# Merge gates of chunks 3 and 4: seven half-size products for all tokens, in place of eight for half of them

## The chip, the cores and the metric

The kernel runs on one core of one Trainium2 chip. The metric is the device time of one execution in microseconds (us), as the median of several runs; lower is better. The engines go by the names that the profile gives them: PE (TensorE, the matmuls; PEld is its weight load), DVE (VectorE), ACT (ScalarE), POOL (GpSimd) and SP (SyncE, which issues most of the DMAs).

## The reference

The reference is one encoder block over 2048 tokens of 1024 channels. Two attention mixers (`ya` and `yb` below) are left as they are; the change lies in the merge gates:

```python
h = rms_norm(x, norm_gain[layer])
proj = h @ w_in[layer]
qa, ka, va, qb, kb, vb, ga, gb, mg = jnp.split(proj, split_idx, axis=-1)
...
br_a = ya @ w_branch_a[layer]
br_b = yb @ w_branch_b[layer]
gates = jax.nn.sigmoid(mg.reshape(bsz, S, N_BRANCHES, D) + b_merge[layer])
merged = gates[:, :, 0] * br_a + gates[:, :, 1] * br_b
x = x + merged @ w_out[layer]
```

`mg` has 2 x 1024 columns: for each of the 1024 output channels two gates, one for each branch. So the merge gates are a product of x (2048 x 1024) with weights of 1024 x 2048.

## The kernel before

**Numbers in two halves.** Values are held as pairs of fp16 numbers, hi and lo, and a product is three matmuls: hi x hi, hi x lo, lo x hi. x lies in SBUF as `XH` and `XL`, with 8 chunks of 128 input channels on the partitions and 2048 tokens in the columns. Each x is used transposed, so a matmul gives 128 output channels by 512 tokens, a quarter of the tokens.

**The stage.** The change lies in the stage of the merge gates, which follows the attention units. The 1024 output channels are 8 chunks `dc`. Five of them are made here, as n = 0 to 4 (chunk n is `DCS[n + 1]`); the other three are made at other places of the kernel. Both gates of a chunk use its raw weights `wraw`, 1024 inputs by 256 columns.

Before anything is multiplied, the weights of a chunk are prepared (`prep`, `w_load` to `w_lo`, lines 188 to 258): four DMAs load them into `wraw`, of which there is only one buffer; POOL multiplies by the norm's gain (L193, four instructions); ACT squares and sums (L235, four); PE adds up the squares over the partitions (L210, one product of 4 columns, which stands in PE's own queue); DVE makes a power of two of the sum, in six small instructions (L217 to L225); ACT makes the hi half (L252) and DVE the lo half (L258).

There are two ways of multiplying:

- `gate_pair(n, q)` makes both gates of a chunk for one quarter q of the tokens: 2 x 24 matmuls of 512 columns (8 input chunks by 3; L333). ACT takes the tanh (L1403), SP stores it into `mgd` in DRAM.
- `gate_group(n)` makes both gates for quarters 0 and 2 at once, by Strassen's scheme in Winograd's form. It sees x as 2 x 2 blocks (quarter 0 or 2, by input chunks 0 to 3 or 4 to 7) and the weights as 2 x 2 blocks (by gate). Eight products of half-size blocks become seven, of 12 matmuls each (L1516), with the sums S1 to S4 of x and T1, T2, T3, N4 of the weights as operands. What comes out of PSUM goes through ACT's copies (L1521), DVE's scaled additions (L1524), POOL's additions (L1527) and ACT's tanh (L1530).

**Sums of x** (`x_sums`, L1435) are made once for quarters 0 and 2: for each pair of channels (c, c + 4) 16 steps, which are four whole values hi + lo (DVE, L1441), four additions or subtractions (DVE, issued from L433), four hi halves (ACT, L1444) and four lo halves (DVE, L1448). They lie in the tiles `wt` (`xsum`, L1424), with the working values in a tile `Y`. **Sums of the weights** (`w_sums`, L1460) overwrite the raw weights: a DVE subtraction (L1483), ACT's hi half (L1484), DVE's lo half (L1480). The last lo half of a chunk is the last reader of `wraw`; only after it can the next chunk be loaded.

**The order of the work.** The order in which instructions are issued is written out by hand. `at(t, f)` puts a step on a heap with a due time t, `job` issues matmuls on a clock of PE (2.6 us for 12) and `until` issues every step whose time has come between them. So the tables `T_P` (start of preparation and of the weights' sums of each chunk), `T_S` (sums of x), `T_O` (blocks of W_out for the kernel's end: `b_load`, L1342, and `b_blocks`, L1352), `T_G`, `T_H`, `T_Y` (loads and splits of Y, the mixers' output, for the next stage) set where a step stands on its engine. At run time each engine takes its instructions in that order and waits where an operand or a buffer isn't ready. The due times don't hold anything back.

In the stage, before, pairs and groups follow in this order (n, q; a group with its number of products): pairs (0, 1) and (0, 3), two products of group 0, pairs (1, 1) and (1, 3), five of group 0, group 1, pairs (2, 1) and (2, 3), groups 2, 3 and 4, then pairs (3, 1), (3, 3), (4, 1), (4, 3). The next stage multiplies Y by the branch weights, with the first matmul `fps<-Y,wh` at L333.

Of the kernel before, what the change touches and what calls it, by code (L numbers as in the profile page):

```python
# [27 lines left out]
OP = mybir.AluOpType  # L28
# [72 lines left out]
T_Y = (2.0, 0.8, 1.6, 1.5, 4.0, 26.0, 0.5, 1.3, 2.1, 1.6, 2.0)  # L101
T_P = ((0, 0.0, 0.03), (1, 3.0, 50.0), (2, 56.0, 75.0), (3, 82.0, 102.0), (4, 108.5, 128.3))
T_O = ((0, 62.0, 84.0), (1, 136.4, 154.0), (2, 136.9, 164.6), (3, 183.9, 190.0))
T_G = (143.4, 174.8, 176.0, 177.4)
T_S = (2.0, 11.0, 0.85, 1.6, 0.75, 1.5, 0.9, 1.3, 0.8)
T_H = (157.4, 2.0, 0.02)
T_GATE = (0.1, 0.1, 0.9, 1.0, 1.0)
T_W = (0.3, 5.5, 1.1, 8.5, 0.9, 15.6, 16.1, 17.0, 0.9, 0.8)
T_B = (20.0, 6.5, 1.55, 0.8)
T_BR = (7.0, 0.95, 20.0, 9.0, 34.0)  # L110
# [13 lines left out]
def block_kernel(tc, x, w_units, w_gate, w_mrg, w_brn, w_out, w_bra, gain, qkg, sink, bias_a, bias_b, b_merge, out):  # L124
# [1150 lines left out]
    ygs, ypool = {}, [(fg, 6, "fg")]  # L1275

    def y_load(c, q):
        ygs[c, q] = ypool[0][0].tile([128, 512], F32, name=ypool[0][2], bufs=ypool[0][1])[:]
        nc.sync.dma_start(out=ygs[c, q], in_=ytd[c][:, 512 * q:512 * q + 512])

    def y_hi(c, q):
        A.activation(YS[q][0][:, c, :], ygs[c, q], AF.Copy, scale=ys[c][:])

    def y_lo(c, q):
        V.scalar_tensor_tensor(YS[q][1][:, c, :], ygs[c, q], ys[c][:], YS[q][0][:, c, :], OP.mult, OP.subtract)
        done.add(("y", c, q))
# [55 lines left out]
    def b_load(j):  # L1342
        if j < 3:
            rv = y0.tile([128, 4, 512], F32, name=f"Y0{1 - j % 2}")[:]
        else:
            rv = raw_tile()[:].rearrange("p a b -> p (a b)")[:, :2048].rearrange("p (a b) -> p a b", b=512)
        for i in range(2):
            for h in range(2):
                nc.sync.dma_start(out=rv[:, 2 * i + h, :], in_=w_out[h, :, 4 * i + j, :])
        bw["out", j] = rv  # L1350

    def b_blocks(t0, j):  # L1352

        b11, b12, b21, b22 = (bw["out", j][:, k, :] for k in range(4))
        sub = {0: (b11, b12, b11), 1: (b12, b22, b12), 3: (b22, b22, b11), 5: (b21, b21, b22)}
        for i, (b, v) in enumerate(((B11, b11), (B22, b22), (B21, b21), (T1, b11), (T3, b12), (T2, b22), (N4, b21))):
            hi, lo = split(wt[0][:, b, j, :], wt[1][:, b, j, :], v, so4)
            at(t0 + T_B[2] * i, hi)
            at(t0 + T_B[2] * i + T_B[3], lambda lo=lo, b=b: (lo(), done.add(("b", j, b))))
            if i in sub:  # L1360
                at(t0 + T_B[2] * i + T_B[3] + .05, lambda o=sub[i]: V.tensor_tensor(*o, OP.subtract))
# [29 lines left out]

    def gate_pair(n, q):
# [5 lines left out]
        for k in range(2):  # L1398
# [11 lines left out]
            at(e + T_GATE[4], store)  # L1410

# [12 lines left out]
    def xsum(i, c):  # L1424
        m = 4 * i + c
        return [wt[k][:, m % 7, 1 + m // 7, :] for k in range(2)]

    def xblock(b, c):
        if b in sidx:
            assert ("xs", sidx[b], c) in done  # L1430
            return xsum(sidx[b], c)
        o = 1024 if b == A22 else 0
        return [X[:, c + (0 if b == A11 else 4), o:o + 512] for X in (XH, XL)]

    def x_sums(t, c):  # L1435
# [4 lines left out]
        def whole(o, ch, tok):  # L1440
            V.tensor_tensor(o, XH[:, ch, tok:tok + 512], XL[:, ch, tok:tok + 512], OP.add)  # L1441

        def hi(v, i):
            A.activation(xsum(i, c)[0], v, AF.Copy, scale=0.25)  # L1444

        def lo(v, i):
            h, l = xsum(i, c)
            V.scalar_tensor_tensor(l, v, 0.25, h, OP.mult, OP.subtract)  # L1448
            done.add(("xs", i, c))
# [39 lines left out]
    def gate_group(n):  # L1489
# [21 lines left out]
        def products(ps, x, bl):  # L1511
            mm = []
            for ch in range(4):
                for k, w in ((0, 0), (1, 0), (0, 1)):
                    i = len(mm)
                    mm.append(lambda ch=ch, k=k, w=w, i=i: T.matmul(  # L1516
                        ps[:], lhsT=weight(bl, ch)[w], rhs=xblock(x, ch)[k], start=(i == 0), stop=(i == 11)))
            return mm
# [10 lines left out]
        def gate(o, v, k, q, late):  # L1529
            at(now[0] + late, lambda: A.activation(o, v, AF.Tanh, bias=bmh[:, 8 * k + dc:8 * k + dc + 1], scale=ims[n][:]))  # L1530
# [26 lines left out]
    for c in range(4):  # L1557
        at(t + T_S[0] + T_S[1] * c, x_sums, t + T_S[0] + T_S[1] * c, c)
# [12 lines left out]
    for c in range(4):  # L1571
        at(t + T_H[0] + T_H[1] * c, y_ahead, c)

# [4 lines left out]
    y_part(t + T_G[3], 0, 2, 0.9)  # L1578
    group0 = gate_group(0)
# [7 lines left out]
    until(clock[0] + T_GATE[4] + .1)  # L1587
# [266 lines left out]
```

## Time and profile before

| what | us |
|---|---|
| three runs | 1916.34, 1916.52, 1917.65 |
| median | 1916.52 |
| profiled execution | 1917.63 |
| its span | 1915.7 |
| PE busy in the span | 1903.7 |
| DVE busy | 1358.8 |
| ACT busy | 1119.7 |
| POOL busy | 842.9 |

The span is the part of the execution that the profile covers. Times in the trace are counted from its start. The stage of the change runs there from 1407.12 (first matmul of pair (0, 1)) to 1601.60 (first matmul of the next stage). Below, s is the time since 1407.12. A row of the order of time on an engine gives start, duration, engine, line, operation, output and inputs with their shapes, how many alike follow each other (x2), and in brackets an idle time before it with what ended it. DVE and ACT overlap instructions that follow each other, so a duration may be longer than the distance to the next start.

### The profile page before, as it was taken

What the parts mean: (1) busy time and instruction counts of PE and PEld (TensorE: products, weight loads), DVE (VectorE), ACT (ScalarE), POOL (GpSimd) and SP (SyncE); (2) the same over time, 40 slices, a digit from 0 to 9 for tenths busy, and PEclk for the clock granted to TensorE, in tenths of its full rate; (3) what the DMA queues carried; (4) which work ended last, traced back from release to release, by engine and by line L of the source; (5) the groups of instructions that cost most, each with busy time, mean ns of one, the idle gap of its engine ahead of it and who ended that gap; (6) DMA issues with size and microseconds to landing.
All of it is one profiled execution on the core that took longest, in us unless ns stands there. A gap on an engine that the chain in (4) does not pass through costs nothing.

```text
span 1915.7 us, 39344 instructions
## 1 busy us (share of the span) xinstructions
PE 1903.7 (99%) x13614; PEld 1195.4 (62%) x13614; DVE 1358.8 (71%) x3513; ACT 1119.7 (58%) x2496; POOL 842.9 (44%) x1848
## 2 busy tenths in 40 slices
PE   8999999999999999999999999999999999999999
PEld 7556666677766688566787667876544444444444
DVE  6668886887767777567776878868686667867312
ACT  7558766786666677566776766666544545323100
POOL 2433444344445655546565565655412211223543
PEclk9999999999999999999999999999999999999999
DMA  7559987797958696678877887767722346788763
GB/s 269 140 90 176 206 162 155 146 192 157 200 98 191 134 194 131 120 155 173 170 134 149 161 176 146 138 118 131 187 76 97 107 154 220 223 253 254 259 229 140
DMA packets 624584, 316.56 MB, mean 165 GB/s; under 512 B 492928, under 2 KB 562176, under 8 KB 623104
## 3 DMA queue, kind: packets, MB, share of 16 engines
q1 hardware_dynamic: 605952, 305.39, 69.2%
q10 hardware_dynamic: 18432, 8.66, 1.9%
q8 instruction: 106, 1.74, 0.4%
q14 instruction: 94, 0.77, 0.2%
HBM read 129.91 MB, written 65.27 MB: 102 GB/s over the span
## 4 chain that ended last, share of the span: by engine, by line
PE 89%; DVE 4%; POOL 2%; issue 2%; ACT 2%; DMA 2%; SPq 0%; DVEq 0%; POOLq 0%; ACTq 0%
PE pj L709 40%; PE pj L333 15%; PE fps L333 11%; PE fps L1721 6%; PE s L879 5%; PE pv L928 4%; PE fps L1516 3%; PE pj L1721 2%; PE pj L1516 1%; PE pj L609 1%; DVE qss L753 0%; DVE pr L894 0%; DMA xt<-in_x_dram 0%; DMA kq<-spl 0%; POOL rw L771 0%
## 5 line engine op out<-in xcount | busy, mean ns | idle before, releaser
L709 PE MATMUL pj<-wh,XL 128*128 128x384 f16 x1792 | 586.1, 327 | 0.0
L709 PE MATMUL pj<-wh,XH 128*128 128x384 f16 x1792 | 584.5, 326 | 1.6 <-DVE vt L741 1.6
L709 PE MATMUL pj<-wl,XH 128*128 128x384 f16 x1792 | 584.7, 326 | 0.0
L709 PEld LDWEIGHTS <-XH 128*128 128x128 f16 x3584 | 410.4, 116 | 152.2 <-issue 2.2
L894 DVE CUSTOM_DVE_ANT_0 pr<-s,b,ubuf 128x256 f32<-128x256 f32 (+3 forms) x512 | 219.1, 465 | 76.7 <-PE s L879 75.1
L709 PEld LDWEIGHTS <-XL 128*128 128x128 f16 x1792 | 207.7, 116 | 70.3 <-issue 1.2
L911 DVE SCALAR_TENSOR_TENSOR p<-pr,p 128x512 f16<-128x512 f32 (+2 forms) x256 | 190.5, 744 | 20.3 <-ACT p L907 20.3
L786 POOL COPY spl<-spl 128x256 f16<-128x256 f16 (+1 forms) x224 | 88.1, 423 | 183.1 <-DVE spl L781 181.6
L726 ACT ACTIVATE rw<-pj 128x256 f32<-128x256 f32 (+1 forms) x224 | 86.6, 386 | 138.8 <-PE pj L709 126.2
L907 ACT ACTIVATE p<-pr 128x512 f16<-128x512 f32 (+2 forms) x256 | 159.2, 622 | 6.2
L333 PEld LDWEIGHTS <-wh 128*128 128x128 f16 x960 | 93.7, 98 | 110.6
L879 PE MATMUL s<-kq 128*128 128x256 f16 (+3 forms) x1168 | 147.8, 254 | 0.0
L928 PEld LDWEIGHTS <-pt 128*128 128x128 f16 x3024 | 125.4, 97 | 35.4 <-DMA pt<-p 0.7
L286 POOL TENSOR_TENSOR rs_t<-rs_y 128x8 f32<-128x8 f32 (+1 forms) x112 | 41.1, 367 | 234.4 <-DVE rs_y L278 185.3
L771 POOL TENSOR_TENSOR rw<-rw,g 128x256 f32<-128x256 f32 (+1 forms) x112 | 90.9, 811 | 109.9 <-DVE rw L765 73.3
L193 POOL TENSOR_TENSOR wraw<-wraw,gn 128x768 f32<-128x768 f32 (+1 forms) x80 | 112.2, 1409 | 55.0 <-DMA wraw<-in_w_mrg_dram 43.2
L928 PE MATMUL pv<-vt,pt 128*128 128x65 f16 (+1 forms) x3024 | 132.7, 192 | 0.3 <-DMA pt<-p 0.3
L879 PEld LDWEIGHTS <-kq 128*128 128x128 f16 x1184 | 101.9, 98 | 41.5
L741 DVE SCALAR_TENSOR_TENSOR vt<-pj,vt 128x128 f16<-128x128 f32 (+1 forms) x224 | 62.1, 277 | 91.2 <-ACT vt L735 87.5
L765 DVE TENSOR_TENSOR rw<-rw,qr 128x512 f32<-128x512 f32 (+1 forms) x112 | 103.8, 927 | 31.8 <-POOL qr L295 31.1
L333 PE MATMUL pj<-XH,gh 128*128 128x512 f16 x320 | 121.3, 379 | 0.0
L333 PE MATMUL pj<-XH,gl 128*128 128x512 f16 x320 | 121.2, 379 | 0.0
(281 smaller groups left out, 3803.2 us busy)
## 6 DMA issues: line engine op xcount, KB each, us to landing
wraw<-in_w_units_dram SPq DMA_DIRECT2D x56, 384.0 KB, 4.7
mtd<-mm SPq DMA_DIRECT2D x56, 256.0 KB, 3.9
M<-mtd SPq DMA_DIRECT2D x8, 1792.0 KB, 9.8
mgd<-fg SPq DMA_DIRECT2D x39, 256.0 KB, 2.1
zd<-z ACTq DMA_DIRECT2D x128, 66.0 KB, 2.5
zz<-zd SPq DMA_DIRECT2D x64, 132.0 KB, 2.8
xt<-in_x_dram SPq DMA_DIRECT2D x16, 512.0 KB, 9.8
gtd<-yo SPq DMA_DIRECT2D x32, 256.0 KB, 3.2
```

The costliest lines, as they stand in the source:

```text
L193: G.tensor_tensor(v, v, gn[:, c0:c0 + 2].unsqueeze(2).to_broadcast([128, 2, n]), OP.mult)
L333: out.append(lambda w=w, xx=xx, ch=ch, i=i: T.matmul(ps[:], lhsT=w[:, ch, c0:c0 + 128], rhs=xx[:, ch, ts], start=(i == 0), stop=(i == n - 1)))
L709: out.append(lambda lhs=lhs, rhs=rhs, ch=ch, k=k: T.matmul(ps[:, :384], lhsT=lhs[:, ch, :], rhs=rhs[:, ch, :], start=(k == 0), stop=(k == ...
L765: V.tensor_tensor(q, q, self.rr[:, :n].unsqueeze(2).to_broadcast([128, n, HD]), OP.mult)
L771: G.tensor_tensor(k, k, GT[un.br][:].unsqueeze(1).unsqueeze(1).to_broadcast([128, 2, un.nk, HD]), OP.mult)
L786: G.tensor_copy(sp[:, i, nh:, :, :], sp[:, i, nq:nh, ::-1, :])
L879: T.matmul(self.sv[j][:, o:o + k1 - k0], lhsT=q[:, h, qo:qo + 128], rhs=kt[:, un.nq + kh + v * un.nk, k0:k1], start=(v == 0), stop=(v == 1))
L894: V.tensor_tensor_reduce(out=self.pv[:, j, self.p0:self.p0 + W], in0=self.sv[j], in1=un.bias[:, self.h0 + j, self.b0:self.b0 + W], scale=I ...
L907: A.activation(self.sp[:, :128 * n], self.pr, AF.Copy, scale=PSC)
L911: V.scalar_tensor_tensor(self.sp[:, 128 * n:], self.pr, PSC, self.sp[:, :128 * n], OP.mult, OP.subtract)
L928: T.matmul(self.po[:, j, :w], lhsT=p[:, n * j + s, :], rhs=un.v[key][:, vh, c0:c0 + w], start=(k == 0 and s == 0), stop=(k == 2 and s == n ...
L1721: mm.append(lambda ch=ch, k=k, w=w, i=i: T.matmul(ps[:, :cols.stop - cols.start], lhsT=m[:, a, ch, k, :], rhs=wt[w][:, b, ch, cols], start ...
```

## The change

Chunks 3 and 4 get a second group each, for quarters 1 and 3 (`p = 1`), and lose their pairs. So for these two chunks all tokens go by seven products. Counted as whole ones of 512 columns there are 24 matmuls fewer in the stage (900 before); 48 of the new groups' are halves of 256 columns, so the number of PE's instructions stays.

- `x_sums`, `xblock` and `xsum` take p. For p = 1 there are 16 more sums, at 16 new places m = 16 to 31. Only 21 places are in `wt`; m = 21 to 31 lie in columns of `XH` and `XL` whose x isn't read any more (`dead` counts the uses). For m = 25 to 28 such a place is two pieces of 256 columns, in two channels; `pieces` cuts every instruction on them in two.
- The places in `wt` are numbered by channel first (4c + i), no longer by sum first (4i + c).
- The working values of Y's quarter 0 (`y_load`) and of block 2 of W_out (`b_load`) also go to such columns, so that the instructions on them (L1339 and L1340, Y's hi and lo halves, now L1361 and L1362) come in halves.
- The order of pairs and groups is a table, `SEQ`; the tables of due times have new numbers.

Lines move: L193 to L196, L210 to L213, L235 to L238, L433 to L436, L1403 to L1437, L1441 to L1489, L1444 to L1496, L1448 to L1501, L1480 to L1533, L1483 to L1536, L1484 to L1537, L1516 to L1573, L1521 to L1579, L1524 to L1582, L1527 to L1585, L1530 to L1589.

```diff
-T_P = ((0, 0.0, 0.03), (1, 3.0, 50.0), (2, 56.0, 75.0), (3, 82.0, 102.0), (4, 108.5, 128.3))
+T_P = ((0, 0.01, 0.01), (1, 4.24, 49.92), (2, 52.84, 74.95), (3, 81.2, 102.03), (4, 107.96, 128.8))
...
+T_X = ((0.11, 13.73, 27.24, 34.11), (48.57, 50.03, 69.09, 119.78))
+SEQ = ((0, 1, 0), (0, 3, 0), (0, 0, 2), (1, 1, 0), (1, 3, 0), (0, 0, 5), (1, 0, 7), (2, 1, 0), (2, 3, 0), (2, 0, 7), (3, 0, 7), (4, 0, 7), (3, 2, 7), (4, 2, 7))
+GROUPS = sorted({(n, q // 2) for n, q, _ in SEQ if q % 2 == 0})
...
+    def pieces(*views):
+        if any(isinstance(v, list) for v in views):
+            return [[v[k] if isinstance(v, list) else v[:, 256 * k:256 * k + 256] for v in views] for k in range(2)]
+        return [views]
...
     def b_load(j):
-        if j < 3:
-            rv = y0.tile([128, 4, 512], F32, name=f"Y0{1 - j % 2}")[:]
+        if j == 2:
+            assert all(dead(0, b, c) for b in (A11, A12) for c in range(4))
+            rv = [x_place(4 + k, 0) for k in range(4)]
...
-    def xsum(i, c):
-        m = 4 * i + c
-        return [wt[k][:, m % 7, 1 + m // 7, :] for k in range(2)]
+    def dead(p, b, c):
+        return uses[p, b, c] == 3 * sum(g[1] == p for g in GROUPS)
+
+    def xsum(p, i, c):
+        m = 4 * c + i + 16 * p
+        if m < 21:
+            return [wt[k][:, m % 7, 1 + m // 7, :] for k in range(2)]
+        if m < 25:
+            return [X[:, m - 21, 1024:1536] for X in (XH, XL)]
+        if m < 29:
+            return [[X[:, 2 * (m - 25) + k, S:S + 256] for k in range(2)] for X in (XH, XL)]
+        return [X[:, m - 29, 1536:2048] for X in (XH, XL)]
...
-        o = 1024 if b == A22 else 0
+        o = 512 * p + (1024 if b == A22 else 0)
         return [X[:, c + (0 if b == A11 else 4), o:o + 512] for X in (XH, XL)]
...
     def gate(o, v, k, q, late):
+            q += p
...
-    for c in range(4):
-        at(t + T_S[0] + T_S[1] * c, x_sums, t + T_S[0] + T_S[1] * c, c)
+    for p in range(2):
+        for c in range(4):
+            b = t + T_X[p][c]
+            at(b, x_sums, b, p, c)
...
-    for n, q in ((0, 1), (0, 3), (group0, 2), (1, 1), (1, 3), (group0, 5), (gate_group(1), 7), (2, 1), (2, 3),
-                 (gate_group(2), 7), (gate_group(3), 7), (gate_group(4), 7), (3, 1), (3, 3), (4, 1), (4, 3)):
-        if isinstance(n, int):
+    for n, q, k in SEQ:
+        if q % 2:
             gate_pair(n, q)
-        else:
-            for _ in range(q):
-                next(n)
+            continue
+        g = groups.setdefault((n, q), gate_group(n, q // 2))
+        for _ in range(k):
+            next(g)
```

What the new numbers move is shown at three places. The first is DVE from the end of the first sums of x on, among the sums of the weights of chunk 1. `wraw` are raw weights, `wl` and `yq` hold lo halves of the weights' sums, `fg` is a gate, `fps` PSUM, `Y` the working values of the sums of x, `wt_21885` and `wt_21886` the two tiles of their hi and lo halves, `ubuf` a scale. Before:

```order
L1448 SCALAR_TENSOR_TENSOR wt_21886<-Y_22232,wt_21885 128x512 x2
L1467 TENSOR_SCALAR ubuf<-ubuf 128x1
L1483 TENSOR_TENSOR wraw<-wraw 128x4x128
L1480 SCALAR_TENSOR_TENSOR wl<-wraw,ubuf,wh 128x4x128
L1483 TENSOR_TENSOR wraw<-wraw 128x4x128
L1524 SCALAR_TENSOR_TENSOR fg<-fps,wt_21885 128x512
L1480 SCALAR_TENSOR_TENSOR wl<-wraw,ubuf,wh 128x4x128
L1483 TENSOR_TENSOR wraw<-wraw 128x4x128
L1480 SCALAR_TENSOR_TENSOR yq<-wraw,ubuf,yq 128x512
L1524 SCALAR_TENSOR_TENSOR fg<-fps,fg 128x512
L1483 TENSOR_TENSOR wraw<-wraw 128x4x128
L1480 SCALAR_TENSOR_TENSOR yq<-wraw,ubuf,yq 128x512
```

After, the end of the same sums of the weights:

```order
L1536 TENSOR_TENSOR wraw<-wraw 128x4x128
L436 TENSOR_TENSOR Y_22328<-Y_22328 128x512
L1489 TENSOR_TENSOR Y_22344<-XH,XL 128x512
L1533 SCALAR_TENSOR_TENSOR wl<-wraw,ubuf,wh 128x4x128
L1501 SCALAR_TENSOR_TENSOR wt_21886<-Y_22328,wt_21885 128x512
L1536 TENSOR_TENSOR wraw<-wraw 128x4x128
L436 TENSOR_TENSOR Y_22344<-Y_22344 128x512
L1582 SCALAR_TENSOR_TENSOR fg<-fps,fg 128x512
L1533 SCALAR_TENSOR_TENSOR yq<-wraw,ubuf,yq 128x512
L1501 SCALAR_TENSOR_TENSOR wt_21886<-Y_22344,wt_21885 128x512
L436 TENSOR_TENSOR Y_22328<-Y_22328 128x512
L1533 SCALAR_TENSOR_TENSOR yq<-wraw,ubuf,yq 128x512
```

The second half's sums of channels 0 and 1 (the rows with `Y` and `wt`, L436, L1489 and L1501) now stand between the sums of the weights, so that the last row, the last reader of `wraw`, has many more instructions ahead of it.

The second is ACT around the squares of chunk 2 (L235, now L238). Before:

```order
L1484 ACTIVATE yq<-wraw,ubuf 128x512 x2
L1530 ACTIVATE fg<-fg,bmh,ubuf 128x512
L1530 ACTIVATE wt_21885<-wt_21885,bmh,ubuf 128x2x256
L1530 ACTIVATE fg<-fg,bmh,ubuf 128x512
L1521 ACTIVATE fg<-fps 128x512
L235 ACTIVATE wl,wsq<-wraw 128x2x256 x2
L1530 ACTIVATE fg<-fg,bmh,ubuf 128x512
L235 ACTIVATE wl,wsq<-wraw 128x2x256 x2
```

After:

```order
L1496 ACTIVATE wt_21885<-Y_22328 128x512
L1589 ACTIVATE fg<-fg,bmh,ubuf 128x512
L1496 ACTIVATE XH<-Y_22344 128x512
L1589 ACTIVATE wt_21885<-wt_21885,bmh,ubuf 128x2x256
L1496 ACTIVATE wt_21885<-Y_22328 128x512
L1589 ACTIVATE fg<-fg,bmh,ubuf 128x512
L1496 ACTIVATE XH<-Y_22344 128x512
L238 ACTIVATE wl,wsq<-wraw 128x2x256 x3
L1579 ACTIVATE fg<-fps 128x512
L238 ACTIVATE wl,wsq<-wraw 128x2x256
```

The hi halves of the new sums (L1496) now stand ahead of the squares, and each of them needs a value of DVE's.

The third is PE at the norm product of chunk 2 (L210, now L213; `ones` is a matrix of ones, `wsq` the sums of squares). Before, in product S3 of group 1:

```order
L1516 LDWEIGHTS wh
L1516 MATMUL fps<-wt_21885,wh 128x512
L210 LDWEIGHTS ones
L210 MATMUL fps<-wsq,ones 128x4
L1516 LDWEIGHTS wh
L1516 MATMUL fps<-wt_21886,wh 128x512
```

After, in product S2 of group 1, with the weights' sum T2 in `yq`:

```order
L1573 LDWEIGHTS yq
L1573 MATMUL fps<-wt_21885,yq 128x512
L213 LDWEIGHTS ones
L213 MATMUL fps<-wsq,ones 128x4
L1573 LDWEIGHTS yq
L1573 MATMUL fps<-wt_21886,yq 128x512
```

The norm product stands 15 matmuls earlier in PE's queue: 316 matmuls of the stage are ahead of it, and 331 were before.

More of the change, by code (lines that the diff above doesn't have):

```diff
@@ L1390, in block_kernel @@
     ims = {}
+    plain = {1: 0, 3: 0}
     def gate_pair(n, q):
@@ L1410, in gate_pair @@
             at(e + T_GATE[4], store)
+        plain[q] += 1
     def prep(t, u):
@@ L1515, in products, with product @@
                     i = len(mm)
-                    mm.append(lambda ch=ch, k=k, w=w, i=i: T.matmul(
-                        ps[:], lhsT=weight(bl, ch)[w], rhs=xblock(x, ch)[k], start=(i == 0), stop=(i == 11)))
+                    def product(ch=ch, k=k, w=w, i=i):
+                        parts = pieces(ps[:], xblock(p, x, ch)[k])
+                        for o, v in parts:
+                            T.matmul(o, lhsT=weight(bl, ch)[w], rhs=v, start=(i == 0), stop=(i == 11 and v is parts[-1][1]))
+                    mm.append(product)
             return mm
```

94 lines of the change are left out of this document (61 added, 33 removed).

## The prediction

> **What bounds the kernel now.** I read the profile's page first, then the stretches by engine, then the order of time on each engine. On the page, the busy line and the chain that ended last say the same: TensorE (PE) works 99% of the span and carries 89% of the chain.
>
> ```profile
> PE 1903.7 (99%) x13614; PEld 1195.4 (62%) x13614; DVE 1358.8 (71%) x3513; ACT 1119.7 (58%) x2496; POOL 842.9 (44%) x1848
> ...
> PE 89%; DVE 4%; POOL 2%; issue 2%; ACT 2%; DMA 2%; SPq 0%; DVEq 0%; POOLq 0%; ACTq 0%
> ```
>
> So a matmul taken away is time taken away, as long as nothing makes PE wait. The stage of the change is read from two PE rows: its first matmul and the first matmul of the next stage.
>
> ```profile
> 1407.12 0.38 PE L333 MATMUL fps<-XH,wh 128*128 128x512 f16 x1
> ...
> 1601.60 0.59 PE L333 MATMUL fps<-Y,wh 128*128 128x512 f16 x2
> ```
>
> The stage lasts 194.5 us. Before, it holds 900 matmuls of 512 columns and four tiny ones, so one takes 0.216 us and PE stands still nowhere. I count time in it as s, microseconds after 1407.12. The stretches (PE, PEld, DVE, ACT, POOL busy) show how close VectorE (DVE) is behind:
>
> ```profile
> 1420.00:1450.00 30.00, 30.00 (x141) 13.53 (x139) 29.64 (x52) 18.20 (x33) 2.12 (x2) 1.00 0.14 54
> 1450.00:1480.00 30.00, 30.00 (x141) 13.62 (x140) 13.18 (x24) 11.98 (x23) 8.78 (x7) 1.00 0.36 123
> ```
>
> While the sums of x are made, DVE is full (29.64 of 30); right behind that it is at 13 of 30. The change puts the second half of the sums there.
>
> **What goes.** Chunks 3 and 4 lose 4 x 48 matmuls of the plain pairs and get 2 x 84 of the groups: 24 fewer, 24 x 0.216 = 5.2 us. Of the 168, 24 come as 48 halves of 256 columns, because four sums lie in two pieces. The end of the kernel has both widths:
>
> ```profile
> L1721 PE MATMUL fps<-wt,M 128*128 128x512 f16 x24 | 5.3, 379 | 0.0
> L1721 PE MATMUL fps<-wt,M 128*128 128x256 f16 x24 | 2.8, 272 | 0.0
> ```
>
> 48 halves cost 5.6 us at this rate against 5.3 for 24 whole ones: between 0 and 0.3, I take 0.1.
>
> **What comes on DVE.** 48 more whole instructions for the sums, four of them cut in two. 36 of them are planned ahead of s 88, in the way of the weights of chunks 2 and 3: the sums of channels 0 and 1 at s 49 to 63, those of channel 2 at s 69 to 82, mixed with the sums of the weights of chunks 1 and 2. DVE works in order, so its queue can be added up.
>
> ```profile
> 1409.28 1.28 DVE L1483 TENSOR_TENSOR Y<-wraw 128x512 f32<-128x512 f32 x2
> ...
> 1419.70 1.52 DVE L433 TENSOR_TENSOR Y<-Y 128x512 f32<-128x512 f32 x1
> ...
> 1443.03 1.29 DVE L1441 TENSOR_TENSOR Y<-XH,XL 128x512 f32<-128x512 f16 x2
> 1444.23 0.68 DVE L1448 SCALAR_TENSOR_TENSOR wt<-Y,wt 128x512 f16<-128x512 f32 x1
> 1444.83 0.69 DVE L433 TENSOR_TENSOR Y<-Y 128x512 f32<-128x512 f32 x1
> ...
> 1450.38 1.47 DVE L1448 SCALAR_TENSOR_TENSOR wt<-Y,wt 128x512 f16<-128x512 f32 x2
> ...
> 1459.28 0.69 DVE L1524 SCALAR_TENSOR_TENSOR fg<-fps,wt 128x512 f32<-128x512 f32 x1
> ...
> 1460.74 1.76 DVE L1483 TENSOR_TENSOR wraw<-wraw 128x512 f32<-128x512 f32 x1
> ...
> 1466.03 0.89 DVE L1480 SCALAR_TENSOR_TENSOR yq<-wraw,ubuf,yq 128x512 f16<-128x512 f32 x1 [0.79 <-ACT yq L1484]
> ...
> 1478.95 0.16 DVE L217 TENSOR_REDUCE wm<-fps 128x1 f32<-128x4 f32 x1 [0.85 <-PE fps L210]
> ...
> 1479.91 0.16 DVE L225 RECIPROCAL ubuf<-ubuf 128x1 f32<-128x1 f32 x1
> ...
> 1492.11 0.75 DVE L1480 SCALAR_TENSOR_TENSOR yq<-wraw,ubuf,yq 128x512 f16<-128x512 f32 x1 [0.79 <-ACT yq L1484]
> ```
>
> From start to start one whole instruction takes 0.60 us (about 0.62 with those that scale by a column), and six small ones 1.2 (1478.95 to past 1479.91). The first half of the sums ended at 1451.85, s = 44.7. It is the same 68 instructions after the change, in other order on a DVE that is full, so I leave 44.7. What slows DVE is GpSimd (POOL):
>
> ```profile
> 1416.70 5.43 POOL L193 TENSOR_TENSOR wraw<-wraw,gn 128x512 f32<-128x512 f32 x4 [24.57 <-DMA wraw<-in_w_mrg_dram]
> ...
> 1460.19 1.75 POOL L1527 TENSOR_TENSOR wt<-fg 128x512 f32<-128x512 f32 x1 [38.07 <-ACT wh L1484]
> ...
> 1470.28 1.04 POOL L193 TENSOR_TENSOR wraw<-wraw,gn 128x512 f32<-128x512 f32 x1 [3.92 <-DMA wraw<-in_w_mrg_dram]
> ...
> 1473.02 2.03 POOL L193 TENSOR_TENSOR wraw<-wraw,gn 128x512 f32<-128x512 f32 x2 [0.17 <-DMA wraw<-in_w_mrg_dram]
> 1478.23 1.27 POOL L1527 TENSOR_TENSOR fg<-fg 128x512 f32<-128x512 f32 x1 [3.18 <-issue]
> ...
> 1496.65 5.38 POOL L193 TENSOR_TENSOR wraw<-wraw,gn 128x512 f32<-128x512 f32 x4 [14.08 <-DMA wraw<-in_w_mrg_dram]
> ```
>
> Beside the gains (L193) at 1416.70 a DVE instruction took 1.52 instead of 0.69, beside the add (L1527) at 1460.19 one took 1.76. I charge DVE 0.8 for each gain and 1.0 for each add that meets it. Against this, on the "SBUF — State Buffer" page, under "Who interferes with whom", the Trainium skill has DVE and GpSimd hold their shared port as an exclusive lock for a whole instruction when DVE reads two SBUF inputs; by it the sum is 2.0 higher (a rival, below), while here four gains beside DVE took 1.36 each instead of 1.04.
>
> **The waits that this makes.** Before a chunk's weights are split, PE itself sums their squares (L210, a 4-column product), and PE waits for ACT's fourth square; the squares wait for POOL's gains, these for the load, and the load for the last DVE instruction that reads the raw buffer of the chunk ahead (the last L1480, now L1533). ACT's and PE's ends of that chain:
>
> ```profile
> 1474.21 0.61 ACT L235 ACTIVATE wl<-wraw 128x512 f16<-128x512 f32 x1
> ...
> 1475.62 0.19 ACT L235 ACTIVATION_READ_ACCUMULATOR wl<-wraw 128x1 f32 x1
> 1475.72 0.58 ACT L1521 ACTIVATE fg<-fps 128x512 f32<-128x512 f32 x1
> ...
> 1502.59 0.19 ACT L235 ACTIVATION_READ_ACCUMULATOR wl<-wraw 128x1 f32 x1
> ```
>
> ```profile
> 1478.72 0.17 PE L210 MATMUL fps<-wsq,ones 128*128 128x4 bf16 x1
> ...
> 1504.64 0.17 PE L210 MATMUL fps<-wsq,ones 128*128 128x4 bf16 x1
> ```
>
> For chunk 2 the last reader ended at 1466.92 (s 59.8), the last square 8.9 us later at 1475.81, and PE came 2.9 later still. For chunk 3: 1492.86 (s 85.7), 9.9 us to 1502.78, and PE 1.9 later. These 2.9 and 1.9 are all the slack there is.
>
> Chunk 2 after. From s 44.7 DVE has ten instructions (5.6 us), stops at s 52.2 for PE's product S2 (the row of 1459.28), then 14 to the last reader, 8.7, and two adds beside them, 2.0: it ends at s 62.9, 3.1 later than before. PE's norm product stands 15 matmuls earlier, 3.2 us, at s 68.3. So PE waits at least 3.1 + 3.2 - 2.9 = 3.4. More: ACT has the squares behind a half of a sum that needs DVE's ninth instruction after the reader, 5.4 us plus two or three beside the gains, s 70.2. From there a half (0.6), three squares at 0.75, a copy (0.6) and the last square (0.8) end at s 74.4: PE has then waited 6.1 in all, some 0.9 of it earlier, in S3 of chunk 0, whose last rows of x now lie where PE has to wait for POOL's add (1460.19 + 1.75 is s 54.8; PE comes at 53.8).
>
> Chunk 3 after. DVE has its column of norms from PE at s 74.4 + 0.4, six small ones 1.2, then 25 whole, four half and two small ones (17.3) and two adds (2.0) up to its last reader: s 95.4, 9.7 later than before. Nearly 9.5 later (between 8.9 and 9.9 above) the last square is done, s 104.9. PE's position is 4 matmuls earlier, s 96.7. PE has waited 8.2 us in all; the second wait contains the first.
>
> Behind that nothing adds: from s 105 DVE's queue is short again, x's second half is done 20 us before chunk 3's second group at s 153, and the loads on SP that wait for PE's last product (Y of quarter 2, with four gate stores and the next stage's loads queued behind) come 3 us after the stage's end, against eight banks of 2.6 us each. The half-sized splits of W_out and Y stand where DVE has gaps; if that cover were gone they cost 19 x 0.3.
>
> **Sum.** The profiled execution took 1917.63 us (span 1915.7 and 1.9 around it), 1.1 above the median 1916.52. 1917.63 - 5.2 + 0.1 + 8.2 = 1920.7, on the median 1919.6: 0.16% slower. About 0.2%, 3.8 us, is what a measurement of this kernel can tell from no change.
>
> **Rivals.** (a) POOL costs DVE nothing: last reader of chunk 2 at s 60.9, ACT's last square at 70.6, PE waits 2.3; chunk 3's reader at 89.6, PE's wait 1.8. In all 2.3: 1913.7. For it: the gain at 1470.28 took 1.04 while DVE was idle; against it: each of the pairs above. (b) No wait at all, because DVE comes earlier through its queue than I add up: -5.1, 1911.4. Against it: 36 whole instructions more before s 88 with 2.9 us of slack. (c) Slower: each POOL operation takes from DVE its whole length alone, 1.27 for four adds and 1.04 for four gains, 9.2 instead of 7.2. Chunk 3's last square is then at s 106.9, the wait 10.2: 1921.6. It decides when POOL's eight operations cost DVE over 7.9. For it: the 1.76 at 1460.74, 1.07 over 0.69. (d) The products are not what they say: excluded, 24 matmuls fewer stand in the order.
>
> **How the numbers follow.** The forecast (a wait of 6 to 9.5, 1917.4 to 1920.9) gets 0.50, of which 0.12 lie above 3.8 us; (a) and what lies between it and the forecast 0.20; (b) 0.12; (c) 0.18. Faster by over 0.2%: 0.12, (b) alone. Slower: 0.18 + 0.12 = 0.30. Within: 0.58. The range leaves (b) and the top of (c) out: 1913.0 to 1921.9.
>
> **What would show it.** Right: PE idle in front of the norm product (now L213), released by ACT, some 5 us for chunk 2 and 2 for chunk 3, and about 1 in front of a group product released by POOL; DVE full from s 52 to 95; the last L1533 of chunk 2 near s 95. Wrong: PE idle under 1.4 us in the stage, or waits elsewhere, above all in the next stage.

## The result, and the profile after

The changed kernel takes 1928.28 us (median of 4 runs, 1927.04 to 1930.85) against 1916.43 before (4 runs, 1916.00 to 1917.65): the ratio is 1.0064, with a 95% interval of 1.0052 to 1.0076. It is slower by 11.9 us, which is more than the range on record allowed.

The page of the changed kernel has the same busy time on PE and 40 us more on DVE:

```profile
PE 1902.3 (99%) x13614; PEld 1195.2 (62%) x13614; DVE 1398.5 (73%) x3594; ACT 1133.8 (59%) x2535; POOL 856.9 (44%) x1852
```

PE's busy time is 1.4 us less, not 5.2. Later rows show why: part of its matmuls ran at a lower clock (behind two waits, 1.7 and 2.7 us lost). The list of PE's waits from the stage's start on was empty before the change. Now it holds (engine, what waits and for whom: us in total, times, longest):

```profile
PE fps L213 <- ACT wl L238: 3.8, 1, 3.8
PE pj L336 <- DVE fg L1718: 3.6, 1, 3.6
PE pj L336 <- DVE Y L1307: 1.7, 2, 0.9
PE fps L336 <- DVE Y L1307: 1.3, 2, 0.9
PE fps L1573 <- POOL wt L1585: 0.6, 1, 0.6
PE fps L336 <- DVE kp L1718: 0.5, 1, 0.5
```

Only the first and the fifth lie in the stage of the gates; the four others lie in the next one, that of Y and the branch weights. Three PE rows give the bounds of both stages: first matmul of the gates, first with Y, first with M, the merged values that are multiplied by W_out at the end. The last matmul ends 145.23 us after the third row in both kernels.

```profile
1404.88 0.38 PE L336 MATMUL fps<-XH,wh 128*128 128x512 f16 x1
...
1600.75 0.59 PE L336 MATMUL fps<-Y,wh 128*128 128x512 f16 x2
...
1777.93 2.32 PE L1782 MATMUL fps<-wt,M 128*128 128x512 f16 x10
```

The third row of the kernel before:

```profile
1767.36 7.93 PE L1721 MATMUL fps<-wt,M 128*128 128x512 f16 x36
```

| | stage of the gates | next stage |
|---|---|---|
| before | 194.48 | 165.76 |
| after | 195.87 | 177.18 |

So the stage of the change itself is 1.4 us longer, and the next, in which no product was changed, 11.4. (The stage starts 2.2 us earlier than before; over all traces of this study that start lies between 1404.5 and 1408.5 with the same code ahead of it, so it says nothing of the change.)

The stretches answer to those shown of before. DVE, which was at 13 of 30 in the second, is now full there, and after it (columns: PE, PEld, DVE, ACT, POOL busy, then PE's granted clock):

```profile
1420.00:1450.00 30.00, 30.00 (x141) 13.61 (x140) 28.94 (x49) 17.23 (x31) 4.04 (x3) 1.00 0.14 53
1450.00:1480.00 30.00, 25.62 (x117) 11.34 (x116) 28.65 (x46) 14.93 (x28) 9.53 (x6) 0.98 0.22 71
1480.00:1500.00 20.00, 20.00 (x90) 8.81 (x88) 20.00 (x35) 11.97 (x22) 3.30 (x2) 0.95 0.32 105
```

**Chunk 2's chain** in the stage of the gates, on DVE, POOL, ACT and PE. The DVE rows are a subtraction and the last reader of chunk 1's raw weights, each beside an addition of POOL's, and the last reader of chunk 2's, for which the load of chunk 3 waits:

```profile
1458.28 1.75 DVE L1536 TENSOR_TENSOR wraw<-wraw 128x512 f32<-128x512 f32 x1
...
1466.09 1.75 DVE L1533 SCALAR_TENSOR_TENSOR yq<-wraw,ubuf,yq 128x512 f16<-128x512 f32 x1
...
1498.37 0.74 DVE L1533 SCALAR_TENSOR_TENSOR yq<-wraw,ubuf,yq 128x512 f16<-128x512 f32 x1
```

```profile
1464.38 2.91 POOL L1585 TENSOR_TENSOR fg<-fg 128x512 f32<-128x512 f32 x1 [4.90 <-DVE fg L1582]
1471.18 1.17 POOL L196 TENSOR_TENSOR wraw<-wraw,gn 128x512 f32<-128x512 f32 x1 [3.89 <-DMA wraw<-in_w_mrg_dram]
1472.67 4.01 POOL L196 TENSOR_TENSOR wraw<-wraw,gn 128x512 f32<-128x512 f32 x3 [0.32 <-DMA wraw<-in_w_mrg_dram]
```

```profile
1477.75 0.19 ACT L238 ACTIVATION_READ_ACCUMULATOR wl<-wraw 128x1 f32 x1
...
1507.81 0.19 ACT L238 ACTIVATION_READ_ACCUMULATOR wl<-wraw 128x1 f32 x1
```

```profile
1477.99 0.16 PE L213 MATMUL fps<-wsq,ones 128*128 128x4 bf16 x1 [3.77 <-ACT wl L238]
...
1508.04 0.16 PE L213 MATMUL fps<-wsq,ones 128*128 128x4 bf16 x1
```

The first of the two readers ends at s 63.0, chunk 2's last square at s 73.1, and PE's norm product goes out with it. Behind the wait PE's matmuls are slow for a while (mean granted clock 0.72 over 6 us, 1.7 us lost):

```profile
1473.60:1478.00 4.40, 0.64 (x4) 0.21 (x3) 4.40 (x5) 4.31 (x11) 2.97 (x3) 1.00 0.40 149
1478.00:1484.00 6.00, 6.00 (x21) 2.40 (x21) 5.83 (x14) 3.99 (x7) 1.35 (x1) 0.72 0.51 139
```

Chunk 3's last square ends at s 103.1. By then PE has lost so much that its norm product comes at the same moment and shows no wait.

**The first loss of the next stage** (1617 to 1626). On SP, four stores of the last group's gates stand in front of the gate loads (kp); on DVE, the last group's last addition (L1582), the first merge (L1718), which waits for such a load, and behind it, among splits of W_out, one of the splits of Y (L1307) for which PE waits:

```profile
1601.68 7.48 SPq L1590 DMA_DIRECT2D mgd<-fg  x4
1609.26 0.38 SPq L1708 DMA_DIRECT2D kp<-mgd  x1
```

```profile
1607.23 0.68 DVE L1582 SCALAR_TENSOR_TENSOR fg<-fps,fg 128x512 f32<-128x512 f32 x1
...
1612.22 0.69 DVE L1718 SCALAR_TENSOR_TENSOR kp<-kp,fps 128x512 f32<-128x512 f32 x1 [1.41 <-DMA kp<-mgd]
...
1618.07 0.74 DVE L1307 SCALAR_TENSOR_TENSOR Y<-yq,ubuf,Y 128x512 f16<-128x512 f32 x1
```

The last product ended before 1601; its addition runs 6 us later, its store after that. Before the change the same load was issued 3.1 us after the stage's end, now 8.5:

```profile
1604.68 0.38 SPq L1647 DMA_DIRECT2D kp<-mgd  x1
```

**The second loss** (1697 to 1712). The splits of Y's quarter 3 stand in a row on DVE in front of the merge (L1718, `fg`) that frees a PSUM bank for PE. They wait for ACT's hi halves (L1303), and these for their loads:

```profile
1696.18 2.06 DVE L1307 SCALAR_TENSOR_TENSOR Y<-yq,ubuf,Y 128x512 f16<-128x512 f32 x3
1698.17 0.68 DVE L1718 SCALAR_TENSOR_TENSOR kp<-kp,fps 128x512 f32<-128x512 f32 x1
1698.76 0.74 DVE L1307 SCALAR_TENSOR_TENSOR Y<-yq,ubuf,Y 128x512 f16<-128x512 f32 x1
1701.73 1.41 DVE L1307 SCALAR_TENSOR_TENSOR Y<-yq,ubuf,Y 128x512 f16<-128x512 f32 x2 [2.23 <-ACT Y L1303]
1703.83 0.75 DVE L1307 SCALAR_TENSOR_TENSOR Y<-yq,ubuf,Y 128x512 f16<-128x512 f32 x1 [0.68 <-ACT Y L1303]
1704.50 0.68 DVE L1718 SCALAR_TENSOR_TENSOR fg<-fg,pj 128x512 f32<-128x512 f32 x1
```

```profile
1700.98 1.37 ACT L1303 ACTIVATE Y<-yq,ubuf 128x512 f16<-128x512 f32 x2 [3.71 <-DMA yq<-ytd]
```

In the kernel before, at most two splits stand there between one merge and the next. Behind this wait of PE's the clock is lower again:

```profile
1705.20:1711.20 6.00, 5.97 (x15) 2.11 (x15) 4.56 (x8) 1.93 (x3) 2.98 (x2) 0.53 0.47 139
```

### The profile page after: what moved, and what is told of

Same layout as the page of the kernel before. It is cut to its first block, busy times and chain, and to the rows that moved or that the text cites. A ratio compares the mean times of both kernels' runs of the same rounds, so it can differ in the third digit from the quotient of the medians.

```text
span 1926.5 us, 39528 instructions
## 1 busy us (share of the span) xinstructions
PE 1902.3 (99%) x13614; PEld 1195.2 (62%) x13614; DVE 1398.5 (73%) x3594; ACT 1133.8 (59%) x2535; POOL 856.9 (44%) x1852
## 5 line engine op out<-in xcount | busy, mean ns | idle before, releaser
L897 DVE CUSTOM_DVE_ANT_0 pr<-s,b,ubuf 128x256 f32<-128x256 f32 (+3 forms) x512 | 219.1, 465 | 76.7 <-PE s L882 74.4
L336 PEld LDWEIGHTS <-wh 128*128 128x128 f16 x832 | 81.5, 98 | 101.6 <-issue 7.8
L196 POOL TENSOR_TENSOR wraw<-wraw,gn 128x768 f32<-128x768 f32 (+1 forms) x80 | 117.7, 1477 | 55.2 <-DMA wraw<-in_w_mrg_dram 43.7
```

The costliest lines, as they stand in the source:

```text
L196: G.tensor_tensor(v, v, gn[:, c0:c0 + 2].unsqueeze(2).to_broadcast([128, 2, n]), OP.mult)
L336: out.append(lambda w=w, xx=xx, ch=ch, i=i: T.matmul(ps[:], lhsT=w[:, ch, c0:c0 + 128], rhs=xx[:, ch, ts], start=(i == 0), stop=(i == n - 1)))
L897: V.tensor_tensor_reduce(out=self.pv[:, j, self.p0:self.p0 + W], in0=self.sv[j], in1=un.bias[:, self.h0 + j, self.b0:self.b0 + W], scale=I ...
```

## The experiments

All start from the changed kernel, but for the last. The stages are measured as above, by three PE rows of each trace; the ratio is to the kernel before on the same chip in the same runs (medians of 1916.2 to 1917.1).

| run | median, us | ratio to before (95%) | gates | next |
|---|---|---|---|---|
| before | 1916.4 | | 194.48 | 165.76 |
| after | 1928.28 | 1.0064 (1.0052 to 1.0076) | 195.87 | 177.18 |
| sums_later | 1934.74 | 1.0092 (1.0075 to 1.0109) | 202.54 | 175.06 |
| stores_act | 1930.05 | 1.0065 (1.0050 to 1.0080) | 196.19 | 176.27 |
| q3_old | 1923.67 | 1.0034 (1.0021 to 1.0047) | 196.41 | 170.77 |
| next_old | 1923.17 | 1.0032 (1.0019 to 1.0045) | 196.51 | 171.10 |
| x_spread | 1926.16 | 1.0052 (1.0037 to 1.0067) | 193.77 | 174.31 |
| wout_late | 1935.95 | 1.0107 (1.0091 to 1.0122) | 196.33 | 183.41 |
| combo | 1928.16 | 1.0064 (1.0048 to 1.0081) | 193.34 | 176.97 |
| tail_plain | 1927.51 | 1.0059 (1.0045 to 1.0073) | 196.79 | 173.60 |
| tb_old | 1924.11 | 1.0039 (1.0025 to 1.0053) | 195.78 | 174.61 |
| combo2 | 1922.51 | 1.0031 (1.0019 to 1.0044) | 190.01 | 175.40 |
| no_sums2 | 1914.32 | 0.9989 (0.9979 to 0.9998) | 189.95 | 167.61 |
| before_plus | 1922.75 | 1.0036 (1.0022 to 1.0050) | 200.97 | 165.76 |

### The sums of x: sums_later, x_spread

```diff
-T_X = ((0.11, 13.73, 27.24, 34.11), (48.57, 50.03, 69.09, 119.78))
+T_X = ((0.11, 13.73, 27.24, 34.11), (84.0, 104.0, 97.0, 119.78))
```

> The second half's sums of x for channels 0, 1 and 2 are due at s 84, 104 and 97 in place of 49, 50 and 69; nothing else is changed. If the sums ahead of the weights' sums hold up PE in the stage of the gates (its norm product waits 3.8 us there, and matmuls at half clock follow), that wait goes, the stage lasts some 190 us in place of 195.9, and the time is 1921 to 1923. Rival: DVE has as much to do in the stage as before, so the wait only moves to a later product of it; the stage stays within 2 us of 195.9 and the time above 1926.

Chunk 2's wait went, and a longer one came at chunk 4's norm product: the stage became 202.5 us and the time 1934.74. The longest of PE's waits:

```profile
PE pj L213 <- ACT wl L238: 9.5, 1, 9.5
```

The rival was right on where it would show, though its 2 us were too few, and the theory on how: sums now stood ahead of the last reader of chunk 3's raw weights, for which chunk 4's load waits, and it ended at s 119.3 (111.1 in the kernel before). So the next run puts them in other places.

```diff
-T_X = ((0.11, 13.73, 27.24, 34.11), (48.57, 50.03, 69.09, 119.78))
+T_X = ((0.11, 13.73, 27.24, 34.11), (57.5, 109.0, 83.0, 136.0))
```

> The second half's sums of x for channels 0 to 3 are due at s 57.5, 109, 83 and 136 (in the changed kernel 49, 50, 69 and 120): each in a stretch of its own, behind the sums of one chunk's weights and ahead of those of the next. Theory: PE waits for a norm product when sums of x stand ahead of the last reader of the raw weights, whichever chunk's; with none there, no norm product waits, the stage of the gates lasts 189.8 to 191, and the time is 1921.5 to 1924. Rival: it is the amount of DVE's work in the stage; then a later chunk's norm product waits as in the run with the sums at 84, 104 and 97, and the time stays above 1926.

Measured 1926.16, at the lower edge of the rival's range. Chunk 2's wait is gone again, and chunk 4's is 3.2 instead of 9.5:

```profile
PE pj L213 <- ACT wl L238: 3.2, 1, 3.2
```

Here the last reader of chunk 3's weights was done at s 114.9. POOL could start chunk 4's gains only behind an addition for the gates, which had waited for a scaled addition (L1582) among the sums of x on DVE, and the four gains, beside sums, took 5.8 us (4.0 in the kernel before):

```profile
1527.58 1.65 POOL L1585 TENSOR_TENSOR fg<-fg 128x512 f32<-128x512 f32 x1 [1.23 <-DVE fg L1582]
1529.19 5.82 POOL L196 TENSOR_TENSOR wraw<-wraw,gn 128x512 f32<-128x512 f32 x4
```

By the numbers, the theory missed in both runs. What they show is that the sums held up the norm product that came behind them, by DVE or by way of POOL. The next stage of x_spread is 2.9 us shorter than the changed kernel's, but PE's waits in it are as long (7.3 us against 7.2, summed before rounding): the difference is the clock, which was 1.00 for the 6 us behind x_spread's second loss and 0.53 in the row above.

### The stage's end: stores_act, wout_late, tail_plain, tb_old

```diff
-            at(now[0] + late + T_S[6], lambda: nc.sync.dma_start(out=whole(mgd[2 * dc + k][:, 512 * q:512 * q + 512]), in_=o))
+            at(now[0] + late + T_S[6], lambda: (nc.scalar if (n, p) == (4, 1) else nc.sync).dma_start(out=whole(mgd[2 * dc + k][:, 512 * q:512 * q + 512]), in_=o))
```

> The four stores of the last group's gates go by ACT's DMA queue, so the loads of gates for the next stage don't stand behind them on SP. Theory: the merge of the next stage's first product on DVE waits for such a load and holds up the splits of Y behind it, which PE waits for at 1617 to 1625. The loads then land near 1604 in place of 1612, at least half of the 3.6 us lost there goes, and the time is 1924.5 to 1926.5. Rival: the splits of W_out's last block fill DVE and ACT there anyway; the waits stay, and the time is 1927.5 to 1929.

Measured 1930.05, 1 us above the rival's range, and PE's waits for Y's splits as they were (3.0 us). The first gate load was issued at 1604.03, two us after the stage's end, and the first merge no longer waited for it; but it ran only 1.3 us earlier against the stage's end, since W_out's splits and the additions of the last group stood ahead of it on DVE. The second load, of the other gate, was issued only at 1612.49, after the last store had landed, and the second merge ran as late as in the changed kernel, 13.8 us after the stage's end. SP's order was not the cause.

```diff
-T_O = ((0, 70.91, 87.97), (1, 128.87, 147.09), (2, 147.22, 150.36), (3, 174.67, 185.08))
+T_O = ((0, 70.91, 87.97), (1, 128.87, 147.09), (2, 147.22, 150.36), (3, 174.67, 190.5))
```

> The splits of W_out's last block are due at 190.5 in place of 185.1, behind the last group's additions on DVE and ACT and not among them. Theory: these splits hold up the additions, with them the last gate stores, the gate loads, and the first merge, behind which Y's splits stand; the last store then goes out 3 to 4 us earlier against the stage's end (8.5 us after it in the changed kernel), the loss at 1617 to 1626 falls by 2 to 3.6, and the time is 1924.5 to 1926.5. Rival: the backlog comes from ahead of the stage's end; the loss stays, or the raw buffer, which comes free later for the next branch weights, makes a new wait of some 4 us: 1928 to 1932.

Measured 1935.95, a miss on the other side. SP came free of the gate stores 1.9 us earlier against the stage's end, and PE's waits at that place did not shrink; the raw buffer came free later, the next branch weights were loaded 26.2 us after the stage's end in place of 19.4 (at 1627.67 and 1620.10), and PE waited 1.2 us for them, the rival's new wait. A longer one, 3.0 us, was for a hi half of Y that stood on ACT behind a hi half of W_out.

```diff
+        if (n, p) == (4, 1):
+            steps = steps[:3] + ((S2, T2, lambda ps: copy(c, ps, 16.0)), (S3, T3, lambda ps: plain_gate(b, ps, 1, 2)),
+                                 (S4, B22, lambda ps: plain_gate(a, ps, 1, 0)), (A22, N4, lambda ps: plain_gate(c, ps, 0, 2)))
         for k, (x, bl, f) in enumerate(steps):
```

(`plain_gate` is ACT's tanh from PSUM and the store.)

> The last four products of the last group (chunk 4, quarters 1 and 3) give their gates by a tanh straight from PSUM, without the scaled additions on DVE and the additions on POOL: three of that group's four gates are left out (other values stand in their place). All products and stores stay. Theory: the last group's chain of additions, which runs to 8 us behind the stage's end, holds back stores, gate loads and first merge, and the loss at 1617 to 1626 comes from it: without the chain the last store goes out within 4 us of the stage's end as before the change, that loss falls by 3 us or more, and the time is 1924 to 1925.5. Rival: DVE is behind anyway, with the splits of W_out and Y; the loss falls by less than 1.5: above 1926.5.

The time, 1927.51, does not tell this run from the changed kernel. Its trace does: the next stage is 173.60 us, 3.6 shorter, and PE waits for Y's splits 1.3 us instead of 3.0. The last store went out 5.5 us after the stage's end, not within 4. Of the 3.6 us, 2.0 are shorter waits and 1.1 matmuls that were slow in the changed kernel's trace; so the theory's mechanism is there, with less than its 3 us.

```diff
-T_B = (18.48, 6.5, 2.0, 1.5)
+T_B = (18.48, 6.5, 1.55, 0.8)
```

> The splits of W_out's blocks come 1.55 apart with the lo half 0.8 behind the hi half, as in the kernel before (2.0 and 1.5 in the changed one). Theory: drawn out, the last block's splits stand behind the first merge, which waits for its gate's load while DVE stands still for some 4 us in all between 1602 and 1613; closer together they use that time, Y's splits come earlier, and the loss at 1617 to 1626 falls by 2 us or more: 1924 to 1926.5. Rival: the merge and its load set the time of Y's splits, not the amount of work; the loss stays: 1927.5 to 1929.

Measured 1924.11, at the lower edge of the theory's range. PE's waits for Y's splits are 1.1 us in place of 3.0, about the theory's 2 us. The next stage is 174.61, 2.6 us shorter, of which 1.0 are waits, since new ones came further on, and 1.6 fewer slow matmuls.

### Y's quarter 3: q3_old, next_old

```diff
-T_Y = (2.34, 0.11, 2.24, 1.3, 4.38, 30.24, 1.38, 1.44, 0.6, 1.4, 1.31)
+T_Y = (2.34, 0.11, 2.24, 1.3, 4.38, 30.24, 0.5, 1.44, 2.1, 1.4, 2.0)
```

> The due times of Y's quarter 3 in the next stage are those of the kernel before (splits 2.1 apart in place of 0.6, loads 2.0 in place of 1.31). Theory: the eight splits stand in a row on DVE ahead of the merges that free PSUM for PE, and with the old times the loss of 6.8 us at 1697 to 1712 goes: 1920.5 to 1922.5. Rival: that loss is the late echo of the one at 1617 to 1625, which has put DVE and SP behind PE; then it stays and the time is above 1926.

Measured 1923.67, 4.6 us less than the changed kernel and 1.2 above the theory's range, with the next stage 6.4 shorter. PE's list of waits has lost its line of 3.6 us and nothing has come for it:

```profile
PE fps L213 <- ACT wl L238: 4.2, 2, 3.8
PE pj L336 <- DVE Y L1307: 2.1, 2, 1.2
PE fps L336 <- DVE Y L1307: 1.3, 2, 0.9
PE fps L1573 <- POOL wt L1585: 0.6, 1, 0.6
PE fps L336 <- DVE kp L1718: 0.5, 1, 0.5
```

The first loss is still there, so the second is no echo of it: it comes from three numbers, of which no run tells one from the other. PE's waits account for 3.3 of the 6.4 us; most of the rest are the slow matmuls behind the wait of 3.6.

```diff
-T_Y = (2.34, 0.11, 2.24, 1.3, 4.38, 30.24, 1.38, 1.44, 0.6, 1.4, 1.31)
+T_Y = (2.34, 0.11, 2.24, 1.3, 4.0, 26.0, 0.5, 1.3, 2.1, 1.6, 2.0)
-T_BR = (15.17, 0.01, 22.76, 8.61, 31.28)
+T_BR = (7.0, 0.95, 20.0, 9.0, 34.0)
```

> All due times of the next stage (Y's quarters 1 to 3, gate loads, branch weights) are those of the kernel before; the stage of the gates stays as changed. If each loss has its own cause, this is the run with the old times of quarter 3 alone, to within 1 us: 1920.5 to 1922.5, and the loss at 1617 to 1625 stays. Rival: the new numbers of the next stage as a whole make both of its losses; then both go and the time is 1917 to 1918.5.

Measured 1923.17, with a next stage of 171.10: as q3_old. The other due times that this run sets back cost nothing. They are not all: the first four numbers of `T_Y` (among them the spacing of quarters 0 and 1, 2.24 for 1.6, and the distance of a lo half from its hi half, 0.11 for 0.8) stayed as changed, and what they cost was not tested.

### Together: combo, combo2

combo joins x_spread, q3_old and wout_late.

> The spread sums, the old times of Y's quarter 3 and the late splits of W_out's last block together. If the three losses of the changed kernel are independent, it gains 5.6, 4.6 and 2 to 3.6 on 1928.3: 1914.5 to 1916, which is below the kernel before. Rival: what was behind one wait shows once it is gone, and half of this is left: 1919 to 1923.

Measured 1928.16, above both ranges: wout_late's new waits were in it (3.0 us for the half of Y, 3.0 for the branch weights). combo2 takes q3_old, tb_old, and once more other places for the sums:

```diff
-T_X = ((0.11, 13.73, 27.24, 34.11), (48.57, 50.03, 69.09, 119.78))
+T_X = ((0.11, 13.73, 27.24, 34.11), (57.5, 122.0, 83.0, 136.0))
```

> The second half's sums due at 57.5, 122, 83 and 136 (channel 1 now behind chunk 4's norm product too), the old times of Y's quarter 3, and the splits of W_out's blocks 1.55 apart. Theory: with no sum ahead of a norm product that hurries, the stage of the gates lasts 189.8 to 191 with PE waiting only the 0.6 us for POOL's addition; the second loss of the next stage is gone and the first smaller: 1914 to 1917. Rival: DVE, full for most of the stage, makes a new wait of 3 us or more: 1918 to 1923.

Measured 1922.51, in the rival's range. The stage of the gates does what the theory says, 190.01 us with no norm product waiting; 4.5 us of the 5.2 that the matmuls are worth are there. And the next stage gives it back, at 175.40 us. The first two lines of PE's waits:

```profile
PE pj L336 <- DVE Y L1307: 5.6, 2, 4.1
PE fps L1573 <- POOL wt L1585: 0.6, 1, 0.6
```

PE arrives earlier at the splits of Y, and they are not ready earlier. No version here that computes the same is faster than the kernel before.

### The sums alone: no_sums2, before_plus

```diff
+        if b in sidx and p:
+            return [X[:, c + 4 * (sidx[b] % 2), 512:1024] for X in (XH, XL)]
         if b in sidx:
...
-    for p in range(2):
+    for p in range(1):
         for c in range(4):
             b = t + T_X[p][c]
```

with the times of q3_old.

> The second half's sums of x are left out: the products of the two added groups that should take them take quarter 1 of x as it lies (whole instead of halves; the number of matmuls by columns is that of the changed kernel), so the gates of quarters 1 and 3 of chunks 3 and 4 are other values. Y's quarter 3 has its old due times. Everything else is as changed: 24 matmuls fewer, the group at the stage's end with its additions, the halves of W_out and Y. Theory: DVE's work on those 48 sums is what costs; without it no norm product waits, DVE is not behind at the stage's end, and the time is 1911.5 to 1914, some 3 us under the kernel before. Rival: the group's tail and the halves make the loss at 1617 to 1626 by themselves; then 3 to 5 us of it stay and the time is 1915.5 to 1918.

Measured 1914.32, faster than before by 0.0011 of it (0.0002 to 0.0021), 0.3 us above the theory's range and below the rival's. PE's whole list:

```profile
PE fps L336 <- DVE Y L1307: 1.3, 2, 0.9
PE fps L1575 <- POOL wt L1587: 0.6, 1, 0.6
```

```diff
+    for c, b in ((1, 47.8), (0, 50.03), (2, 69.09), (3, 119.78)):
+        at(t + b, idle_sums, t + b, c)
     for j, b, d in T_O:
```

(`idle_sums` issues the 16 steps of `x_sums`, with values that stay in `Y`; made from the kernel before. Channels 0 and 1 have changed places, and the first sums are due 0.8 us earlier than in the changed kernel.)

> The kernel before, with as much work on DVE (48 instructions of 512 columns) and ACT (16) as the second half's sums bring, on working tiles alone and at the same due times; its results go nowhere. Products, order and tables are those before. Theory: this alone makes norm products wait in the stage of the gates, 3 to 7 us in all, and leaves DVE behind at its end: 1920 to 1926. Rival: the work fits into DVE's gaps (it stood still for 4 of 10 us there), and the changed kernel's waits come from its earlier norm products and its new order: 1916 to 1918.

Measured 1922.75, which is 6.1 more than its kernel before in the same runs (1916.65). Norm products and group products wait, 4.1 us in all, and the stage is 6.5 longer:

```profile
PE fps L210 <- ACT wl L235: 2.5, 2, 2.3
PE fps L1516 <- ACT wt L1530: 1.3, 1, 1.3
PE pj L1516 <- POOL wt L1527: 0.3, 1, 0.3
```

The theory's second half did not come: the next stage is 165.76, to the hundredth that of before. So in the old order nothing of this reaches the next stage.

## Why the prediction was wrong

**What bounds the kernel: held.** 24 matmuls fewer were worth what the sum says. In no_sums2 and combo2 the stage is 4.5 us shorter with nothing in it but 0.6 us of waiting for POOL. The halves cost next to nothing: the stage is 190.01 with them (combo2) and 189.95 without (no_sums2).

**What comes on DVE, and the first waits: held.** The last reader ahead of chunk 2's load was forecast for s 62.9 and ended at s 63.0, with 1.07 lost beside each of POOL's additions and 0.7 beside each gain (0.8 was charged). The last square was forecast for s 74.4 and came at 73.1, chunk 3's for 104.9 and came at 103.1. The wait for POOL's addition cost 0.8 from matmul to matmul, 0.6 of it idle (0.9 forecast). The stage's loss was forecast at 8.2 and is 6.5: 195.87 less the 189.3 of 876 matmuls at 0.216, less the halves' 0.1. As the prediction read the Trainium skill's exclusive lock ("SBUF — State Buffer", "Who interferes with whom"), the end would have come later, near rival (c)'s. In the trace DVE lost 1.07 and 0.7 where POOL alone needs 1.27 and 1.04, so not a whole POOL instruction each time.

**How it was lost: not as told.** The prediction let the second wait contain the first. In the trace 4.4 us are idle time of PE, and most of the rest is matmuls at the lower granted clock behind it, which no term of the sum held. This mis-sized no total, since both come to the same late square: in tb_old no matmul was slow behind the same wait of 3.8 us, chunk 3's norm product waited 1.6 us instead, and the stage was as long (195.78).

**"Behind that nothing adds": this is the step that failed.** 11.4 us came behind that, in the next stage, and they alone carry the time out of the range. It is what the prediction itself had named as a sign of being wrong, waits in the next stage. It failed in two places:

- The loads on SP were said to come 3 us after the stage's end, because they wait for PE's last product. They wait for the last group's stores, and these for its additions on DVE, and came after 8.5. Eight PSUM banks were named as cover; the cover that counted was DVE's queue, where Y's splits stand behind merges that wait for these loads and behind splits of W_out. What was missing is a sum of DVE's work over the whole stage: the row of sums over the 240 us from the stage's start says 170.5 us before and 208.1 after. A DVE that full has few of the gaps left in which the prediction put halves and additions.
- The due times of Y's quarter 3 were changed in the same diff, and the prediction put no price on them. With the three old numbers, splits 2.1 apart in place of 0.6 among them, 6.4 us of the 11.4 were gone (q3_old): 3.3 of waiting, and most of the rest slow matmuls.

The sums of those rows, of before and of after:

```profile
sum 240.00, PE 240.00 PEld 108.79 DVE 170.52 ACT 124.83 POOL 42.35; mean PE 10.00 PEld 4.53 DVE 7.11 ACT 5.20 POOL 1.76
```

```profile
sum 240.00, PE 232.44 PEld 106.71 DVE 208.09 ACT 134.67 POOL 55.31; mean PE 9.69 PEld 4.45 DVE 8.67 ACT 5.61 POOL 2.30
```

**The account.** From the stages of before, no_sums2, q3_old and after: fewer matmuls with the group's tail, the halves and the other due times, -4.5 in the gates' stage and +1.9 in the next; the second half's sums, +6.5 and +3.2; quarter 3's due times, -0.5 and +6.4. In all +12.8, against 1928.28 - 1916.43 = 11.9 by the medians. Each stage's figure is of one trace, and the slow matmuls in it, up to 3.2 us in a stage of these four, can be there in one trace and not in another (below). The sums' share is shown from both sides: taking them out of the changed kernel with quarter 3's old times brings 9.4 us by the medians (1923.67 to 1914.32; 8.9 if each is taken against the kernel before in its own runs), putting their work alone into the kernel before costs 6.1. The difference between the two lies in the next stage, where the sums cost 3.2 us only together with the rest of the change. Both runs move ACT's 16 hi halves together with DVE's 48 instructions; no run tells the two apart.

**What stays open.** How the first loss of the next stage divides between the last group's additions, W_out's drawn-out splits and the sums. PE's waits for Y's splits there are 3.0 us in the changed kernel (3.4 in q3_old), and 1.1 to 1.3 when any one of the three is left out or tightened (tail_plain, tb_old, no_sums2), so they overlap. That the 1.9 left in no_sums2 come from the group's tail and the halves is argued, not shown; the due times that no run set back are a rival.

**Rivals.** (a) and (b) were too hopeful in the stage, (c) was too high there and, by its time of 1921.6, the nearest. None of them had its place behind the stage.

## What to carry to other kernels

A saving on the bound engine has to be weighed against the work that makes it possible, over the whole stretch in which that work can be done: here 5.2 us of matmuls cost 29 us of DVE (48 instructions at 0.6; DVE's busy time in before_plus, 1387.9, is 29.1 above that of the kernel before), and a DVE that is busy for 87% of 240 us passed its delay on from each of the four places that the work was given. Where a change swaps tables of due times, every row of them is part of the change, also those of stages that it does not speak of; check each for what it puts in front of the instruction that frees a buffer.

## What the runs showed of the hardware

The granted clock of PE did not follow from the length of a wait alone. The wait for chunk 2's norm product is 3.77 us in the changed kernel and in tb_old; behind it the mean clock over 6 us was 0.72 in the one (the row shown above) and 1.00 in the other. A wait of 2.32 us (before_plus) was followed by slow matmuls from 1.1 us later on, 0.43 us apart in place of 0.22, and one of 3.24 us (x_spread) by none. The stretch behind the wait of tb_old, and that of before_plus:

```profile
1477.50:1483.50 6.00, 6.00 (x29) 2.76 (x29) 5.83 (x14) 3.98 (x7) 1.35 (x1) 1.00 0.52 128
```

```profile
1481.30:1485.00 3.70, 3.69 (x13) 1.49 (x13) 3.53 (x11) 2.40 (x4) 1.96 (x2) 0.66 0.11 40
```

The Trainium skill ("TensorE: Matmul & The Clock Gate", Part 1) gives an idle window of about 3.4 us for the fall to half the clock, and says that the window runs freely. A wait of 3.77 us may or may not hold such a window whole, which is in keeping with the first pair, though no run here shows the window. A wait of 2.32 us can't hold one, and cost clock all the same; the figure alone doesn't give that.
